# A state-space layer whose TensorE work is put in a written order, with the small products gathered in clusters and the decay differences made by broadcast loads

## The chip, the cores and the metric

The kernel runs on one core of one Trainium2 chip. The metric is the device time of one launch in microseconds (us). PE is TensorE, DVE VectorE, ACT ScalarE, POOL GpSimd, SP the engine that issues most loads.

## The reference

A network of two layers serves two requests with the same weights: a prompt of 256 tokens without history, and eight sequences of 16 tokens with caches, 384 tokens of width 1024 in all. The first layer (a short convolution beside attention) and both feed-forward parts are untouched here. The second layer is a Mamba-2 mixer: 32 heads of 64 in four groups, a state of 128, a convolution of width 4. It computes, cut to what matters:

```python
def odd_mixer(h, ...):
    z, xbc, dt_raw = split(h @ w_in)
    xbc = silu(causal_dwconv(xbc, conv_state, conv_w, conv_b))
    xs, bm, cm = split(xbc)
    dt = softplus(dt_raw + dt_bias)
    y, h_last = ssd_scan(xs, dt, -exp(a_log), bm, cm, ssm_state, chunk)
    y = (y + d_skip * xs) * silu(z)
    y = rms_norm(y per group) * norm_w
    return y @ w_out, ...

def ssd_scan(x, dt, a, bmat, cmat, h0, chunk):       # per chunk of 64, or a whole sequence of 16
    cum = cumsum(dt * a)
    decay = exp(where(tri, cum[q] - cum[s], -inf))   # per head, q and s in the chunk
    mix = (c[q] . b[s]) * decay * dt[s]
    y_intra = mix @ x
    states = sum over s of b[s] * exp(cum[last] - cum[s]) * dt[s] * x[s]
    h = exp(cum[last]) * h + states                  # from chunk to chunk
    y_inter = exp(cum[q]) * (c[q] . h_in)
```

## The kernel before

Features or tokens lie on the 128 partitions. Each dense product is made of three TensorE products (`three`): the weight and the activation are split into a rounded high part and a low rest (`wh` and `wl`, `Hh` and `Hl`), and high by high, low by high and high by low are added up in PSUM. Lines 413 to 415 of the profile are these three. Weights arrive in blocks of 128 x 1024 (512 KB) in one fixed sequence on SP's queue into three buffers (`raw`). ScalarE copies a block to `wh` (line 294), DVE subtracts to get `wl` (line 288); a block feeds 24 dense products of 384 columns. `W.take` hands out the pieces in the order of the packed file, so that order and the order of the dense products in the program have to agree.

PSUM has eight banks. In the SSM layer three of them (`pmm`) take dense products and five (`paux`) the small ones.

The layer goes through its four groups g of eight heads. For each group there are:

- *conv*: six tiles of 128 channels (`conv4`): 24 dense products named xbc each, then `pad` (DVE takes them out of PSUM), a first step of the convolution `c` on ScalarE, three on DVE, and the silu on ScalarE. Two tiles give B and C, four give x.
- *turns*: `cb` (C by B) and `bT` (B transposed) for three blocks of 128 tokens; twelve transposes xT turn x to `xt`, tokens on partitions.
- *decays*: the differences cum[q] - cum[s] of a group, four tiles of 128x512 (`td`, two blocks of 128 prompt tokens by two halves of four heads). Here they are TensorE products sg of `tdr` (made by DVE) and `ck`; ScalarE then takes relu and exp.
- *scan*: for each of three blocks of tokens `mix` (DVE: decay by cb), `xdt` (DVE) and `xw` (GpSimd), sixteen small products y of 64 columns, S (states of a prompt block) and yi (the part from the earlier state). The third block holds the eight sequences: their states `h0` (256 KB each) are loaded, give eight products yi, and new states hn, four of which fill four small banks at a time.
- *gate*: z, 72 dense products of 512 columns; `y` times silu(z), a mean square over the group, the scaling `rg`, then twelve transposes yT, split to `yh` and `yl`.
- *out*: op, 96 dense products of 384 columns, added to the residual X.

Ahead of the first group stand the step sizes: six transposes `dtt`, a softplus of some twenty small DVE instructions to `dt` and `dA`, and the products E, cT and sgS, which sum dA over the chunk.

The order in which each engine runs its instructions is made by a scheduler at build time: it places an instruction when its inputs are ready by its own costs, in program order as a tie-break. A `Fill` feeds dense products of the next group's conv, of z and of the last group's out between the scan's small ones: `fill(n)` behind a small step lets n x `FILL_O[g]` steps of three dense products go.

```python
FILL_O = (1.4, 1.5, 1.5, 0.6)
def __call__(self, n=1):
    self.due += n * self.ratio
    while self.due >= 1:
        self.due -= 1
        next(self.gen, None)
```

In the profile a name with a number, such as `y__5073`, is one buffer's use; `h__` are the loaded states, and after the group's first products S1 too.

Of the kernel before, what the change touches and what calls it, by code (L numbers as in the profile page):

```python
# [18 lines left out]
P = 128  # L19
# [8 lines left out]
FILL_O = (1.4, 1.5, 1.5, 0.6)  # L28
# [55 lines left out]
def _pack(x):  # L84
# [150 lines left out]
def build(nc, tc, d, stop=None):  # L235
    ctx = ExitStack()
    V, S, G, T = nc.vector, nc.scalar, nc.gpsimd, nc.tensor
# [101 lines left out]
    class Weights:  # L339
        def __init__(self):  # L340
            self.tiles, self.made, self.raw, self.pos = {}, 0, None, 0

            self.gain, t = {}, 32 + 3 * NF + 6
            for g in range(5):
                t += (6 if g < 3 else 0) + (4 if g < 4 else 0)
# [566 lines left out]
    o1 = od.enter_context(tc.tile_pool(name="o1", bufs=2))  # L912
    sts = o0.tile([P, 24, NB, 3], F32, name="sts")
# [79 lines left out]
    def channels(g):  # L993

        Bg, Cg = t512("B", 1, (P, NT)), t512("C", 2, (P, NT))
        yield from conv4(16 + g, Bg)
        yield from conv4(20 + g, Cg)
# [21 lines left out]
        xt = t512("xt", 2, (P, 3, 512))  # L1019
        for i in range(4):  # L1020
            xf = t512("sq", 2, (P, NT))
            yield from conv4(4 * g + i, xf)
            ps = paux("xT")
            for b in range(3):
                T.transpose(ps[:, b * P:(b + 1) * P], xf[:, b * P:(b + 1) * P], ident)
            act(xt[:, :, i * P:(i + 1) * P], ps[:, :NT].rearrange("p (b n) -> p b n", n=P), AF.Copy)
        return Cg, Cm, CB, Bt, Bm, xt
# [116 lines left out]
    class Gate:  # L1144
# [26 lines left out]
        def part(self, b):  # L1171
            y = self.ys[b]
            tt(y, y, self.got["z"][:, b, :], ALU.mult)
            if self.late:
                with tc.high_priority():
                    self.turn(b)
# [87 lines left out]
```

## Time and profile before

| | before |
|---|---|
| median of 3 runs | 1079.92 us (1077.25 to 1080.81) |
| profiled execution | 1079.71 us |
| its span in the trace | 1077.9 us |
| mean granted TensorE clock | 0.989 |
| SSM layer, first xbc to first product of the last feed-forward part | 459.16 to 795.70 us |

The span runs from the first to the last instruction of the trace; the execution's own time has the launch around it. A row of the timeline gives the start, the duration, engine, line and operation, output and inputs, partitions and elements, and in brackets how long the engine had idled and which engine's instruction let it go. In a row of grouped instructions the count, the busy sum in us and the mean of one in ns stand behind the shapes. A PE row's duration reaches past the start of the next one, since products overlap in the array; what one costs in a row of them is the distance of the starts.

### The profile page before, as it was taken

What the parts mean: (1) busy time and instruction counts of PE and PEld (TensorE: products, weight loads), DVE (VectorE), ACT (ScalarE), POOL (GpSimd) and SP (SyncE); (2) the same over time, 40 slices, a digit from 0 to 9 for tenths busy, and PEclk for the clock granted to TensorE, in tenths of its full rate; (3) what the DMA queues carried; (4) which work ended last, traced back from release to release, by engine and by line L of the source; (5) the groups of instructions that cost most, each with busy time, mean ns of one, the idle gap of its engine ahead of it and who ended that gap; (6) DMA issues with size and microseconds to landing.
All of it is one profiled execution on the core that took longest, in us unless ns stands there. A gap on an engine that the chain in (4) does not pass through costs nothing.

```text
span 1077.9 us, 16678 instructions
## 1 busy us (share of the span) xinstructions
PE 1054.0 (98%) x6332; PEld 972.6 (90%) x6332; DVE 739.3 (69%) x1321; ACT 476.5 (44%) x741; POOL 158.2 (15%) x377
## 2 busy tenths in 40 slices
PE   9999999999999999999899999999899999999998
PEld 6788899999999999988768689785899999999998
DVE  7968557777677644478889769677787677765332
ACT  6344334544444433357445545552454444444221
POOL 0030000100000000023454432324001000010000
PEclk9999999999999999999899899999899999999999
DMA  8542543344444444432444435436334344344441
GB/s 280 153 151 76 158 131 126 125 129 126 125 130 124 138 122 133 121 108 97 147 160 163 137 117 187 149 125 218 101 123 137 125 130 125 130 121 149 137 147 42
DMA packets 47944, 146.07 MB, mean 136 GB/s; under 512 B 5720, under 2 KB 7976, under 8 KB 47864
## 3 DMA queue, kind: packets, MB, share of 16 engines
q1 hardware_dynamic: 41976, 132.55, 38.9%
q10 hardware_dynamic: 4608, 8.39, 2.0%
q0 software_dynamic: 1280, 4.06, 1.0%
q8 instruction: 50, 0.82, 0.3%
q14 instruction: 30, 0.25, 0.1%
HBM read 131.61 MB, written 13.37 MB: 135 GB/s over the span
## 4 chain that ended last, share of the span: by engine, by line
PE 45%; DVE 8%; ACT 2%; issue 1%; DMA 1%; ACTq 0%; DVEq 0%; POOL 0%
PE fg L413 3%; PE fg L414 3%; PE fd L414 3%; PE fd L415 3%; PE fd L413 3%; PE fg L415 3%; PE fa L415 3%; PE fa L414 3%; PE fa L413 3%; DVE c L291 2%; PE z L413 2%; PE xbc L414 2%; PE z L414 2%; PE xbc L415 2%; PE xbc L413 2%; PE z L415 2%
## 5 line engine op out<-in xcount | busy, mean ns | idle before, releaser
L288 DVE TENSOR_TENSOR wl<-raw,wh 128x1024 fp32r<-128x1024 f32 (+1 forms) x205 | 252.1, 1231 | 134.7 <-ACT wh L294 134.0
L294 ACT ACTIVATE wh<-raw 128x1024 fp32r<-128x1024 f32 (+1 forms) x205 | 216.1, 1055 | 232.7 <-PE fd L414 95.0
L413 PE MATMUL fg<-Hh,wh 128*128 128x384 f32 x352 | 118.5, 337 | 1.1 <-DVE pad L288 0.8
L414 PE MATMUL fg<-Hl,wh 128*128 128x384 f32 x352 | 118.7, 337 | 0.0
L413 PE MATMUL fa<-Hh,wh 128*128 128x384 f32 x352 | 118.6, 337 | 0.0
L414 PE MATMUL fa<-Hl,wh 128*128 128x384 f32 x352 | 118.4, 336 | 0.1
L415 PE MATMUL fa<-Hh,wl 128*128 128x384 f32 x352 | 118.4, 336 | 0.0
L415 PE MATMUL fg<-Hh,wl 128*128 128x384 f32 x352 | 118.3, 336 | 0.0
L413 PE MATMUL fd<-hh,wh 128*128 128x384 f32 x352 | 118.3, 336 | 0.0
L415 PE MATMUL fd<-hh,wl 128*128 128x384 f32 x352 | 118.3, 336 | 0.0
L414 PE MATMUL fd<-hl,wh 128*128 128x384 f32 x352 | 118.3, 336 | 0.0
L291 DVE SCALAR_TENSOR_TENSOR c<-pad,prm,c 128x400 f32<-128x400 f32 (+1 forms) x160 | 103.5, 654 | 6.9 <-ACT c L294 5.1
L413 PEld LDWEIGHTS fg<-Hh,wh 128*128 128x128 f32 x352 | 66.2, 188 | 1.7 <-ACT R L294 1.1
L413 PE MATMUL xbc<-Hh,wh 128*128 128x384 f32 x192 | 66.4, 346 | 0.7 <-DVE X L288 0.7
L414 PE MATMUL xbc<-Hl,wh 128*128 128x384 f32 x192 | 66.7, 347 | 0.0
L414 PEld LDWEIGHTS fa<-Hl,wh 128*128 128x128 f32 x352 | 66.2, 188 | 0.5 <-DVE Hl L291 0.4
L415 PEld LDWEIGHTS fg<-Hh,wl 128*128 128x128 f32 x352 | 66.2, 188 | 0.1
L415 PE MATMUL xbc<-Hh,wl 128*128 128x384 f32 x192 | 66.3, 345 | 0.0
L413 PEld LDWEIGHTS fa<-Hh,wh 128*128 128x128 f32 x352 | 66.2, 188 | 0.1
L414 PEld LDWEIGHTS fg<-Hl,wh 128*128 128x128 f32 x352 | 66.2, 188 | 0.1
L414 PEld LDWEIGHTS fd<-hl,wh 128*128 128x128 f32 x352 | 66.2, 188 | 0.0
L415 PEld LDWEIGHTS fa<-Hh,wl 128*128 128x128 f32 x352 | 66.2, 188 | 0.0
(808 smaller groups left out, 2141.2 us busy)
## 6 DMA issues: line engine op xcount, KB each, us to landing
raw<-w SPq DMA_DIRECT2D x219, 512.0 KB, 3.5
kc<-kc SPq DMA_DIRECT2D x8, 256.0 KB, 3.5
vc<-vc SPq DMA_DIRECT2D x8, 256.0 KB, 3.0
X<-x SPq DMA_DIRECT2D x8, 192.0 KB, 3.8
o_y<-X SPq DMA_DIRECT2D x8, 192.0 KB, 2.7
o_v<-vt POOLq DMA_DIRECT2D x3, 256.0 KB, 2.5
o_k<-kraw POOLq DMA_DIRECT2D x3, 256.0 KB, 3.3
cst<-cst SPq DMA_DIRECT2D x1, 617.0 KB, 6.0
```

Source lines behind the costliest of these rows:

```text
L288: (eng or V).tensor_tensor(out=out, in0=a, in1=b, op=op)
L291: V.scalar_tensor_tensor(out=out, in0=a, scalar=s, in1=b, op0=op0, op1=op1)
L294: S.activation(out, a, f, **kw)
L413: T.matmul(out, lhsT=ah, rhs=bh, start=start, stop=False)
L414: T.matmul(out, lhsT=ah, rhs=bl, start=False, stop=False)
L415: T.matmul(out, lhsT=al, rhs=bh, start=False, stop=stop)
```

## The change

- `FILL_O` and the filling of the SSM layer go. A wrapper around TensorE keeps products and transposes in the program's order (`keep_in_program_order`) from the first turn of x to the end of the layer, and the program is written out as that order.
- For each of the first three groups the small products stand in five clusters with dense runs between: yT of the group before, S and y of all three blocks (`within`) / 24, 48 or 72 xbc / yi, cb, bT (`before`, `turn_bc`) / 24 xbc / four hn / 24 xbc / four hn / z (behind 24 more xbc in group 2) / xT / 48 xbc or 96 op. The last group alternates with pieces of z and op.
- The weight blocks are packed in the new order: B and C of a group apart from its x.
- The decays: cum is copied from PSUM (`cumK` per token, `cumQ` per head), `cumQ` goes to a DRAM tile `rows`, and each td is loaded by a DMA on SP's queue that repeats four rows of 128 on all partitions (256 KB written); GpSimd subtracts `cumK`. `tdr`, `cq`, `ck` and the sixteen sg go.
- The mix of the two prompt blocks is made in place in td; `xt` has one buffer, and yi and S1 are kept in it. Adding yi to y and the skip product move to GpSimd for three groups (the skip product was there before). The mean square's scratch is `yi`.

```diff
-FILL_O = (1.4, 1.5, 1.5, 0.6)
...
-    def chan(g):
-        fm(wi, (4096 + P * g, 4608 + P * g))
+    def bc(which, g):
+        fm(wi, (4096 + 512 * which + P * g,))
+    def xs(g):
         fm(wi, range(2048 + 512 * g, 2560 + 512 * g, P))
...
-    chan(0)
+    bc(0, 0), bc(1, 0), xs(0), bc(0, 1), bc(1, 1)
     for g in range(4):
+        if g == 2:
+            bc(0, 3), bc(1, 3)
         if g < 3:
-            chan(g + 1)
+            xs(g + 1)
         tm(wi, 512 * g)
+        if g == 0:
+            bc(0, 2), bc(1, 2)
         if g:
             out(g - 1)
...
+    class Tensor:
+        keep = False
+        def matmul(self, *a, **kw):
+            ins = nc.tensor.matmul(*a, **kw)
+            if self.keep:
+                tc.keep_in_program_order(ins)
...
+    T = Tensor()
...
-    cq = o0.tile([P, 2, P], F32R, name="cq")
-    ck = o0.tile([P, 2, P], F32R, name="ck")
-    V.memset(f32(cq[64:128, :, :]), 1.0)
-    V.memset(f32(ck[0:64, :, :]), 1.0)
+    cumK = o0.tile([P, 64], F32, name="cumK")
+    V.tensor_copy(cumK, ps[:, 0:64])
...
-    cs = ps[0:32, 0:256].rearrange("p (b q) -> p b q", q=P)
-    act(cq[0:32, :, :], cs, AF.Copy)
-    tt(cq[32:64, :, :], cs, f32(cq[0:32, :, :]), ALU.subtract)
-    act(ck[64:96, :, :], cs, AF.Copy, scale=-1.0)
-    V.tensor_scalar_mul(ck[96:128, :, :], f32(cq[32:64, :, :]), -1.0)
+    cumQ = o1.tile([32, 256], F32, tag="pad", name="cumQ")
+    V.tensor_copy(cumQ, ps[0:32, 0:256])
+    rows = dram.tile([2, 32, P], F32, name="rows")
+    nc.sync.dma_start(out=rows.rearrange("b h q -> h b q"), in_=cumQ.rearrange("h (b q) -> h b q", q=P))
...
+        return Cg, Cm, CB, Bt, Bm
+    def turn_x(xs):
+        xt = t512("xt", 1, (P, 3, 512))
+        for b in range(3):
             ps = paux("xT")
-            for b in range(3):
-                T.transpose(ps[:, b * P:(b + 1) * P], xf[:, b * P:(b + 1) * P], ident)
-            act(xt[:, :, i * P:(i + 1) * P], ps[:, :NT].rearrange("p (b n) -> p b n", n=P), AF.Copy)
-        return Cg, Cm, CB, Bt, Bm, xt
+            for i in range(4):
+                T.transpose(ps[:, i * P:(i + 1) * P], xs[i][:, b * P:(b + 1) * P], ident)
+            act(xt[:, b, :], ps, AF.Copy)
+        return xt
...
     def decays(g):
-        sg, out = [], []
+        out = []
         for b in range(2):
             for hf in range(2):
                 c0 = 8 * g + 4 * hf
-                td = o1.tile([P, 4, P], F32R, tag="tdr", name="tdr", bufs=2)
-                tt(td, f32(cq[:, b, :]).unsqueeze(1).broadcast_to([P, 4, P]),
-                   C("hsel")[:, c0:c0 + 4].unsqueeze(2).broadcast_to([P, 4, P]), ALU.mult)
-                ps = paux("sg")
-                T.matmul(ps, lhsT=ck[:, b, :], rhs=td.rearrange("p h q -> p (h q)"), start=True, stop=True)
                 dec = t512("td", 4, (P, 4, P))
-                act(dec.rearrange("p h q -> p (h q)"), ps, AF.Relu, scale=-1.0)
+                nc.sync.dma_start(out=dec, in_=rows[b, c0:c0 + 4, :].partition_broadcast(P))
+                tt(dec, dec, cumK[:, 32 * b + c0:32 * b + c0 + 4].unsqueeze(2).broadcast_to([P, 4, P]), ALU.subtract, G)
+                act(dec, dec, AF.Relu, scale=-1.0)
                 out.append(dec)
         for dec in out:
             act(dec, dec, AF.Exp, scale=-1.0)
...
+    class Group:
...
+            self.mix, self.xdt, self.xw, self.ys = [decs[0:2], decs[2:4]], [], [], []
+            for b in range(2):
+                for half in self.mix[b]:
+                    tt(half, half, self.CB[:, b, :].unsqueeze(1).broadcast_to([P, 4, P]), ALU.mult)
...
+                xdt = t512("xdt", 3)
+                tt(heads(xdt[:, :]), x3, bc64(self.col(dt, b)), ALU.mult)
...
+                tt(heads(xw[:, :]), x3, bc64(self.col(wdt, b)), ALU.mult, G)
...
+        def skip(self):
...
+                y = t512("y", 5)
+                tt(heads(y[:, :]), heads(self.xt[:, b, :]), bc64(prr("dsk", 32)[:, self.h8]), ALU.mult, G)
+                self.ys.append(y)
...
+        def within(self):
...
+            for b in range(3):
+                if b < 2:
+                    ph = paux("S")
+                    T.matmul(ph, lhsT=self.Bt[:, b, :], rhs=self.xw[b], start=True, stop=True)
+                    if b == 0:
...
+                py = paux("y")
...
+                        T.matmul(py[q, 64 * h:64 * h + 64], lhsT=self.mix[b][h // 4][:, h % 4, q],
+                                 rhs=self.xdt[b][:, 64 * h:64 * h + 64], start=True, stop=True)
+                tt(self.ys[b], self.ys[b], py, ALU.add)
+            self.h0 = []
+            for bb in range(NB):
+                h0 = t512("h0", 8)
+                nc.sync.dma_start(out=h0, in_=d["h0"][bb, g])
+                self.h0.append(h0)
...
+        def before(self, late):
...
+                yi = self.xt[:, b, :]
+                tt(heads(yi), heads(pi[:, :]), bc64(self.col(E, b)), ALU.mult)
+                tt(self.ys[b], self.ys[b], yi, ALU.add, None if late else G)
...
+        def states(self, par):
...
+            ph = [paux("hn") for _ in range(4)]
...
+                T.matmul(ph[i], lhsT=self.Bm[rows, par, :], rhs=self.xw[2][rows, :], start=True, stop=True)
...
+                tt(heads(h0[:, :]), heads(h0[:, :]), bc64(E[:, o:o + 8]), ALU.mult, G)
+                tt(h0, h0, ph[i], ALU.add)
+                nc.scalar.dma_start(out=d["o_hs"][bb, self.g], in_=h0)
...
+        def part(self, b, zs):
...
+            tt(y, y, zs[:, b, :], ALU.mult)
+            act(t512("yi", 1), y, AF.Square, accum_out=self.ssq[:, b:b + 1])
...
     decs = decays(0)
-    cur, out = run(channels(0)), None
-    for g in range(4):
-        got = {}
-        def beside_scan():
-            if g < 3:
-                got["next"] = yield from channels(g + 1)
-            got["z"] = yield from project_z()
-            if g:
-                yield from add_out(*out)
-        fill = Fill(beside_scan(), FILL_O[g])
-        gate = Gate(fill, got, g == 3)
-        decs = scan(fill, gate, g, decs, *cur)
-        if "z" not in got:
-            fill.rest()
-        gate(None, None)
-        now = gate.end()
-        fill.rest()
-        out, cur = now, got.get("next")
...
+    T.keep = True
+    xt = turn_x(xs)
+    grp = Group(0, decs, bc_, xt)
+    grp.skip()
+    Cn = conv_bc(1, 1)
+    xs = [conv_x(1, 0)]
+    out = None
+    for g in range(3):
+        grp.within()
+        decs = decays(g + 1)
+        if g == 2:
+            Bn, Cn = conv_bc(0, 3), conv_bc(1, 3)
+        if g:
+            xs = [conv_x(g + 1, 0)]
+        if g < 2:
+            xs.append(conv_x(g + 1, 1))
+        grp.before(False)
+        bc_ = turn_bc(g + 1, Bn, Cn)
+        if g == 2:
+            xs.append(conv_x(g + 1, 1))
+        else:
+            xs.append(conv_x(g + 1, 2))
+        grp.states(0)
+        xs.append(conv_x(g + 1, len(xs)))
+        grp.states(1)
+        if len(xs) < 4:
+            xs.append(conv_x(g + 1, 3))
+        zs = run(project_z())
+        gate = Gate(grp.ys, False)
+        for b in range(3):
+            gate.part(b, zs)
+        xt = turn_x(xs)
+        gate.factor()
+        nxt = Group(g + 1, decs, bc_, xt)
+        if g == 0:
+            Bn, Cn = conv_bc(0, 2), conv_bc(1, 2)
+        else:
+            run(add_out(*out, None))
+        for b in range(3):
+            gate.turn(b)
+        out, grp = gate.y2, nxt
+        grp.skip()
+    grp.within()
+    z = project_z()
+    steps(z, 12)
+    grp.before(True)
+    zs = steps(z)
+    gate = Gate(grp.ys, True)
+    for b in range(3):
+        gate.part(b, zs)
+    grp.states(0)
+    op = add_out(*out, None)
+    steps(op, 12)
+    grp.states(1)
+    gate.turn(0)
+    steps(op, 12)
+    for b in (1, 2):
+        gate.turn(b)
+    steps(op)
     nc.gpsimd.dma_start(out=d["o_sm"], in_=osm)
-    run(add_out(*out))
+    run(add_out(*gate.y2, gate.factor()))
+    T.keep = False
```

TensorE at the end of group 0 and the start of group 1 (yT turns the gated y of group 0, S and y belong to group 1, xbc to a later conv) has this order before the change:

```order
L415 MATMUL xbc<-Hh,wl 128x384
L596 MATMUL yT<-cst,y__4976 128x128 x4
L413 MATMUL xbc<-Hh,wh 128x384
L596 MATMUL yT<-cst,y__5073 128x128 x4
L414 MATMUL xbc<-Hl,wh 128x384
L596 MATMUL yT<-cst,y__5267 128x128 x4
L1084 MATMUL y<-xdt__5641,mix__5647 64x64 x16
L1123 MATMUL S<-xw__5643,Bt__5132 128x512
L415 MATMUL xbc<-Hh,wl 128x384
```

Each turn is followed by a dense product, and S and y are spread between dense ones. After the change TensorE has at that place:

```order
L249 MATMUL xbc<-Hh,wl 128x384
L254 MATMUL yT<-cst,y__5023 128x128 x4
L254 MATMUL yT<-cst,y__5025 128x128 x4
L254 MATMUL yT<-cst,y__5027 128x128 x4
L249 MATMUL S<-xw__5598,Bt__5292 128x512
L249 MATMUL y<-xdt__5596,td__5200 64x64 x8
L249 MATMUL y<-xdt__5596,td__5204 64x64 x8
L249 MATMUL S<-xw__5602,Bt__5292 128x512
L249 MATMUL y<-xdt__5600,td__5208 64x64 x8
L249 MATMUL y<-xdt__5600,td__5212 64x64 x8
L249 MATMUL y<-xdt__5604,mix__5608 64x64 x16
L249 MATMUL xbc<-Hh,wh 128x384
```

Dense products no longer stand between the transposes, and the y products of blocks 0 and 1 read td itself; the yT rows follow a run of dense ones in which no other small product stands.

ScalarE around the decays of the next group (td: relu and exp; wh: weight copies; c4: first step of a conv; sq and xf: its silu) has this order before the change, in group 0, for group 1:

```order
L294 ACTIVATE td__5221<-sg_5219 128x512
L294 ACTIVATE td__5227<-sg_5225 128x512
L294 ACT_TABLE_LOAD
L294 ACTIVATE td__5221<-td__5221 128x512
L294 ACTIVATE wh_5436<-raw_5434 128x1024
L294 ACTIVATE td__5233<-sg_5231 128x512
L294 ACTIVATE td__5239<-sg_5237 128x512
L294 ACTIVATE td__5227<-td__5227 128x512
L294 ACTIVATE td__5233<-td__5233 128x512
L294 ACTIVATE td__5239<-td__5239 128x512
L294 ACTIVATE c4_5295<-pad4_5288,prm_74 128x408
L294 ACTIVATE c4_5346<-pad4_5339,prm_74 128x408
```

Relu reads the PSUM bank of sg there. After the change ScalarE has, in group 1, for group 2:

```order
L315 ACTIVATE td__5808<-td__5808 128x512
L315 ACT_TABLE_LOAD
L315 ACTIVATE td__5808<-td__5808 128x512
L315 ACTIVATE td__5812<-td__5812 128x512
L315 ACTIVATE td__5816<-td__5816 128x512
L315 ACTIVATE td__5820<-td__5820 128x512
L315 ACTIVATE td__5812<-td__5812 128x512
L315 ACTIVATE wh_5957<-raw_5955 128x1024
L315 ACTIVATE td__5816<-td__5816 128x512
L315 ACTIVATE td__5820<-td__5820 128x512
L315 ACTIVATE c4_5867<-pad4_5860,prm_74 128x408
L315 ACTIVATE wh_6023<-raw_6021 128x1024
```

Relu now reads td itself instead of PSUM, and the first conv step c4 stands behind all eight steps of the decays.

DVE at the end of the step-size chain (lp to dA; c4 and pad4 are conv work) has this order before the change:

```order
L291 SCALAR_TENSOR_TENSOR c4_4739<-pad4_4732,prm_74,c4_4739 128x408
L291 SCALAR_TENSOR_TENSOR lp_4583<-lp_4581,lr_4571 128x96
L291 SCALAR_TENSOR_TENSOR c4_4739<-pad4_4732,prm_74,c4_4739 128x408
L291 SCALAR_TENSOR_TENSOR lp_4585<-lp_4583,lr_4571 128x96
L291 SCALAR_TENSOR_TENSOR c4_4739<-pad4_4732,prm_74,c4_4739 128x408
L291 SCALAR_TENSOR_TENSOR lp_4587<-lp_4585,lr_4571 128x96
L291 SCALAR_TENSOR_TENSOR c4_4804<-pad4_4797,prm_74,c4_4804 128x408
L288 TENSOR_TENSOR wl_4923<-raw_4920,wh_4922 128x1024
L291 SCALAR_TENSOR_TENSOR lu_4589<-lp_4587,lz_4569 128x96
L291 SCALAR_TENSOR_TENSOR c4_4804<-pad4_4797,prm_74,c4_4804 128x408
L291 SCALAR_TENSOR_TENSOR dt_4533<-lu_4589,mxx_4591 128x96
L291 SCALAR_TENSOR_TENSOR c4_4804<-pad4_4797,prm_74,c4_4804 128x408
```

Conv steps and a wl alternate with the chain. After the change DVE has there:

```order
L312 SCALAR_TENSOR_TENSOR lp_4587<-lp_4585,lr_4573 128x96
L312 SCALAR_TENSOR_TENSOR lp_4589<-lp_4587,lr_4573 128x96
L312 SCALAR_TENSOR_TENSOR lu_4591<-lp_4589,lz_4571 128x96
L312 SCALAR_TENSOR_TENSOR dt_4535<-lu_4591,mxx_4593 128x96
L312 SCALAR_TENSOR_TENSOR dA_4536<-dt_4535,ea_4596 128x96
L309 TENSOR_TENSOR h0__4599<-dA_4536,cst_75 128x256
L309 TENSOR_TENSOR h0__4621<-dA_4536,cst_75 128x512
L995 COPY cumK_4611<-E_4601 128x64
L309 TENSOR_TENSOR wdt_4538<-E_4537,dt_4535 128x96
L1000 COPY cumQ_4616<-cT_4613 32x256
L309 TENSOR_TENSOR pad4_4678<-xbc_4647,R_79 128x256
L309 TENSOR_TENSOR pad4_4678<-xbc_4647,R_79 128x8x16
```

The conv steps that stood between the chain's instructions now stand behind it, cumK, wdt and cumQ.

More of the change, by code (lines that the diff above doesn't have):

```diff
@@ L341, in __init__ @@
             self.tiles, self.made, self.raw, self.pos = {}, 0, None, 0
[L343 removed]
+            self.gain, t = {}, 32 + 3 * NF + 8
             for g in range(5):
[L345 removed]
+                t += (4 + 4 + 2, 4 + 4, 2 + 4 + 4, 4, 0)[g]
                 if g:
@@ L991, in build, with conv_x, conv_bc, turn_bc @@
     act(decS, ps, AF.Exp)
[L993 to L997, printed above, removed]
+    def conv_x(g, i):
+        out = t512("xf", 4, (P, NT))
+        run(conv4(4 * g + i, out))
+        return out
+    def conv_bc(which, g):
+        out = t512("BC"[which], 1 + which, (P, NT))
+        run(conv4(16 + 4 * which + g, out))
+        return out
+    def turn_bc(g, Bg, Cg):
         ps = paux("cb")
@@ new lines, in build @@
+    decs = decays(0)
+    bc_ = [conv_bc(0, 0), conv_bc(1, 0)]
+    xs = [conv_x(0, 0)]
+    bc_ = turn_bc(0, *bc_)
+    xs += [conv_x(0, i) for i in (1, 2, 3)]
+    Bn = conv_bc(0, 1)
+    T.keep = True
[18 more added lines that the diff above has]
+            xs.append(conv_x(g + 1, 1))
+        else:
+            xs.append(conv_x(g + 1, 2))
[6 more added lines that the diff above has]
+        gate = Gate(grp.ys, False)
+        for b in range(3):
+            gate.part(b, zs)
[4 more added lines that the diff above has]
+            Bn, Cn = conv_bc(0, 2), conv_bc(1, 2)
+        else:
+            run(add_out(*out, None))
+        for b in range(3):
+            gate.turn(b)
+        out, grp = gate.y2, nxt
+        grp.skip()
```

190 lines of the change are left out of this document (71 added, 119 removed).

## The prediction

> **What bounds the kernel now.** I read the page first, then the chain of waits of TensorE, the windows of the SSM stage and its timeline.
>
> ```profile
> span 1077.9 us, 16678 instructions
> PE 1054.0 (98%) x6332; PEld 972.6 (90%) x6332; DVE 739.3 (69%) x1321; ACT 476.5 (44%) x741; POOL 158.2 (15%) x377
> ```
>
> TensorE is busy for 98% of the span, so only its idle time, its slow time and its order can be won. The change touches the stage between these two rows:
>
> ```profile
> 459.16 0.41 PE L413 MATMUL xbc<-Hh,wh 128*128 128x384 f32 x1 [0.74 <-DVE X L288]
> ...
> 795.70 0.34 PE L413 MATMUL fa<-Hh,wh 128*128 128x384 f32 x1
> ```
>
> 795.70 − 459.16 = 336.5 us. The next view gives busy us and count of PE, PEld, DVE, ACT, POOL, then TensorE's granted clock; the three lines behind it show TensorE alone in stretches at half clock.
>
> ```profile
> 459.00:796.00 337.00, 323.11 (x1988) 269.62 (x1989) 270.64 (x492) 171.42 (x305) 111.55 (x166) 0.97 0.42 142
> 517.40:524.20 6.80, 6.18 (x40) 0.50 0.86 308
> 613.00:619.80 6.80, 6.78 (x13) 0.50 0.73 231
> 756.30:763.10 6.80, 5.00 (x20) 0.50 0.64 208
> ```
>
> DVE works 271 of 337 us, 80%: whatever TensorE waits for is mostly queued there. At half clock the busy 6.18 + 6.78 + 5.00 = 18.0 us hold 9.0 us of full-speed work, so 9.0 us are lost. What TensorE waits for:
>
> ```profile
> PE y L1084 <- DVE mix__5075 L288: 3.2, 2, 2.5
> PE yT L596 <- DVE h__7491 L288: 2.5, 1, 2.5
> PE yT L596 <- DVE yi__7567 L288: 1.4, 1, 1.4
> PE sg L1042 <- DVE tdr L288: 1.3, 2, 0.7
> PE xT L1025 <- ACT sq__5358 L294: 1.2, 1, 1.2
> ...
> PE cb L1001 <- ACT C__6481 L294: 0.2, 1, 0.2
> ```
>
> The twelve rows of that answer, less X's 0.7 that lies ahead of the stage, come to 13.3 us.
>
> **What the change takes away.** Stepping between kinds of work and the products that go:
>
> ```profile
> L1042 PE MATMUL sg<-tdr,ck 128*128 128x512 f32 x16 | 7.0, 466 | 1.3 <-DVE tdr L288 1.3
> 561.58 0.39 PE L415 MATMUL z<-wh,Hl 128*128 128x512 f32 x1
> 561.81 0.34 PE L413 MATMUL xbc<-Hh,wh 128*128 128x384 f32 x1
> 561.98 0.34 PE L414 MATMUL xbc<-Hl,wh 128*128 128x384 f32 x1
> ...
> 574.14 0.66 PE L596 MATMUL yT<-cst,y__4976 128*128 128x128 f32 x4
> 574.55 0.42 PE L413 MATMUL xbc<-Hh,wh 128*128 128x384 f32 x1
> 574.81 0.60 PE L596 MATMUL yT<-cst,y__5073 128*128 128x128 f32 x4
> 577.60 0.74 PE L415 MATMUL xbc<-Hh,wl 128*128 128x384 f32 x1
> 578.18 0.34 PE L413 MATMUL xbc<-Hh,wh 128*128 128x384 f32 x1
> ```
>
> - Starts of dense products lie 0.17 us apart at 384 columns, 0.23 at 512. The sixteen sg (512 columns, overlapped in the pipe) are worth 16 × 0.23 = 3.7 us; their summed busy time, 7.0, is the upper end.
> - A dense step beside small products costs more: 574.55 to 574.81 is 0.26 (0.09 over), 577.60 to 578.18 is 0.58 (0.41 over). My mean over the stage is 0.19 a run of small products. There are 64 such runs between dense ones; the new order has 28. 36 × 0.19 = 7.0 us; ends 36 × 0.09 = 3.2 and 36 × 0.41 = 14.8.
> - The new-state products hn wait for free PSUM banks inside a run, which the waits do not list:
>
> ```profile
> 744.70 1.14 PE L1108 MATMUL hn<-xw__7384,Bm__6616 32*128 32x512 f32 x8
> 612.40 2.79 PE L1108 MATMUL hn<-xw__5967,Bm__5134 32*128 32x512 f32 x3
> ```
>
> A clean set of four (eight passes) takes 1.14; the second row shows three passes taking 2.79. The eight sets take 15.5 us start to start against 8 × 1.07, so 7.0 us of waiting.
>
> With all waits gone the stage would be 336.5 − 3.7 − 7.0 − 13.3 − 7.0 − 9.0 = 296.5 us. DVE also loses sixteen tdr products; the small products themselves are not fewer or shorter. The moved weight blocks are the same bytes on the same queue: nothing.
>
> **What it puts back.** With a fixed order TensorE cannot pass a late small product, so every lateness behind the cover is a wait.
>
> *Startup.* The dt chain on DVE runs from the transposes to dA:
>
> ```profile
> 469.75 0.86 PE L473 MATMUL dtt<-cst,dts 128*128 128x32 f32 x6
> 470.65 0.57 DVE L291 SCALAR_TENSOR_TENSOR dx<-dtt,r,prm 128x32 f32<-128x32 f32 x3 [2.11 <-PE dtt L473]
> 474.03 1.22 DVE L288 TENSOR_TENSOR wl<-raw,wh 128x1024 fp32r<-128x1024 f32 x1
> 476.04 0.74 DVE L323 RECIPROCAL lr<-la 128x96 f32<-128x96 f32 x1
> 485.30 0.29 DVE L291 SCALAR_TENSOR_TENSOR dA<-dt,ea 128x96 f32<-128x96 f32 x1
> 485.64 0.41 PE L966 MATMUL E<-dA,cst 128*128 128x32 f32 x2 [0.91 <-DVE dA L291]
> ```
>
> Now 81 xbc (14.1 us) cover the 15 us; then 72 xbc stand ahead of E in all, 32 of them behind dtt, so TensorE is dry at 470.4 + 32 × 0.174 = 476.0. On DVE only three wl (3 × 1.2) and no conv work stand among the chain's own 5 us of small instructions; with ScalarE's steps it ends near 479.8. Wait 3.8, and 1.2 more until pad4_4678, now behind cumK, wdt and cumQ on DVE, frees a bank: 5.0. Ends: 0, if DVE were ready, and 9.3, if the chain kept its 15 us. The half clock followed idles of 2.5 us in the stretches above, so I add 2.5.
>
> *Decays, three groups.* The broadcast into td (256 KB) can start only when the y products have read the old td; then four GpSimd subtractions in a row, and ScalarE's relu and exp stand ahead of wh and of the next conv's first step, so conv and evacuation on DVE come late, hn's banks and the next cb with them.
>
> ```profile
> 514.17 2.02 POOL L288 TENSOR_TENSOR y__5267<-xt__4764,prm 128x512 f32<-128x512 f32 x1
> 621.12 1.04 POOL L288 TENSOR_TENSOR h__6181<-h__6181,E 128x512 f32<-128x512 f32 x1 [6.89 <-PE yi L1101]
> 530.97 1.28 ACT L294 ACT_TABLE_LOAD   x1
> 532.26 0.64 ACT L294 ACTIVATE td__5221<-td__5221 128x512 f32<-128x512 f32 x1
> 536.14 0.68 DVE L288 TENSOR_TENSOR mix__5647<-td__5221,CB__5125 128x512 f32<-128x512 f32 x1
> 554.92 1.53 DVE L288 TENSOR_TENSOR y__5267<-y__5267,yi__5578 128x512 f32<-128x512 f32 x1
> h__5377<-h SPq DMA_DIRECT2D x1, 256.0 KB, 3.8
> ```
>
> Chain: 3.8 (a 256 KB load) + 4 × 1.04 + relu 0.64 + table 1.28 + 4 × 0.64 = 12.4 us behind the last y. Cover in dense work: 24 xbc (4.2 us) ahead of the second cluster in group 0, 48 and 72 in the next two, and 24 xbc between each of the following clusters. The lower end is that none of it shows (0), the upper that the 12.4 us less 4.2 show in every group (24.6). On SP's queue td's loads stand ahead of raw and h0 loads and hold them while they wait for y; three raw buffers of 24 dense products each cover 3 × 4.2 = 12.5 us, so I count nothing for it, and nothing for their 4 MB beside the stage's 337 us × 142 GB/s = 48 MB. I take 7.0 over the three, what hn waits for banks now, and 3.5 for the second cluster of group 2, whose cb needs a C convolved just then.
>
> *From group 0 to group 1.* z ends at 561.81 and its yT starts at 574.14: 12.3 us of gate, mean square and scale, covered by 69 xbc. Afterwards xT (1.1) and 48 xbc (8.3) cover 9.4, while DVE has the mix and xdt products of the next group and the same wl as well: I put yT 1.7 later than now (a wl of 1.2 and a small step), at 14.0, so 4.6 late, and a half-clock stretch (6.8 × 0.5 = 3.4) behind it: 8.0. Ends: 2.9, if yT keeps its 12.3 and the clock holds, and 12, if two more products of 1.53 stand ahead of it and the clock falls. Groups 1 and 2 have 96 op (16.7 us): nothing.
>
> *Smaller.* xT of group 0 waits for ScalarE's last silu, 1.0 (as sq__5358 above, 1.2); op's wh behind the scaling of y on ScalarE, 2 × 0.9; cluster 1 wants five aux banks in a row, 3 × 0.5; the last gate 1.0, in place of the 2.5 and 1.4 above. Together 5.3. GpSimd's added sums hide under 48 or more dense products.
>
> Sum: 7.5 + 7.0 + 3.5 + 8.0 + 5.3 = 31.3. Stage 296.5 + 31.3 = 327.8, gain 8.7. The profiled execution took 1079.71 (median 1079.92, 0.02% off): 1079.7 − 8.7 = **1071 us**.
>
> The Trainium skill, "SBUF — State Buffer" (section on SBUF's two separate sides), says that VectorE with two SBUF inputs and a GpSimd operation that reads SBUF take a shared port in turn, as a lock for the whole instruction. The trace agrees in size: the same 128x512 product takes 0.68 or 1.53 on DVE, 1.04 or 2.02 on GpSimd. By that rule the new GpSimd work is a loss for DVE too; the third rival prices it from the rows.
>
> **Rivals.**
> - *Cushion.* Three mm banks and three weight buffers absorb all but the startup and the turn to group 1: 296.5 + 7.5 + 8.0 = 312.0, gain 24.5, 1055 us. For it: ScalarE is only half busy (171 of 337). Against: DVE at 80%.
> - *Half clock in each group.* The clusters are long runs of short products and each ends in a wait; if each of three groups drops the clock once, 3 × 3.4 = 10.2: 1081 us, no change. For it: all three stretches above began at such places. The Trainium skill, "TensorE: Matmul & The Clock Gate" (Why this matters), puts the drop at idle gaps over some 3 us; this trace shows it dropped after 2.5, and the measurement decides; by that rule this rival would be dearer to reach and the charge of 2.5 at the startup would stay.
> - *GpSimd late* (slower). Each subtraction takes 2.02, not 1.04, since DVE works beside it: the chain is 4 × 0.98 = 3.9 later in three groups, 11.8, and with the clock falling in each, 10.2, it is 1071 + 22 = 1093 us. It decides from 8.7 / 3 = 2.9 a group without the clock, a subtraction of 1.77. For it: 271 us of DVE work; against: sixteen tdr leave DVE.
>
> **How the numbers follow.** Forecast 0.42 (1061 to 1077), cushion 0.18, half clock 0.16, GpSimd late 0.24. Below 1052 I leave 0.08, above 1089 0.12, so the range is 1052 to 1089: its ends lie near the cushion and between the two slow cases. A change under 0.3% (3.2 us) can hardly be told from none here. Faster 0.60, same 0.16, slower 0.24.
>
> **What the profile after would show.** No sg and fewer than 30 small runs between dense ones; an idle of 3 to 5 us ahead of E, released by dA; yT of group 0 late by 4 to 5 us behind rg; hn sets longer than 1.14 or a cb that waits for C; and the clock at 0.50 behind the longest of these. I am wrong if td's broadcasts land much later than 3.8 us (they share SP's queue with the weights), if GpSimd's subtractions are near 2 us, or if the idle sum stays under 15 us.

## The result, and the profile after

The changed kernel takes 1117.07 us (median; 1114.3 to 1119.4) against 1080.11 in the runs beside it: ratio 1.0346, 95% interval 1.0316 to 1.0377. It is 37 us slower, where 8.7 us less were forecast (1071). The page of the changed kernel:

```profile
span 1117.5 us, 16676 instructions
PE 1059.1 (95%) x6316; PEld 979.4 (88%) x6316; DVE 750.8 (67%) x1297; ACT 478.3 (43%) x737; POOL 183.0 (16%) x399
PEclk9999999999999999988988899899999999999999
```

TensorE has 16 products fewer, the sg, and yet idles 5% instead of 2% of a longer span. The SSM stage runs from 461.20 to 835.44 us, 374.2 us against 336.5 (the remaining 2 us lie ahead of it, where runs of the unchanged part differ by as much). The first line is its window (start and end, length, busy us and count of PE, PEld, DVE, ACT and POOL, TensorE's clock, share and GB/s of the DMA engines); then TensorE alone in the seven stretches at half clock:

```profile
459.00:836.00 377.00, 329.95 (x1983) 277.58 (x1982) 282.50 (x468) 174.20 (x301) 137.24 (x188) 0.92 0.43 139
480.40:490.60 10.20, 8.45 (x27) 0.51 0.55 189
508.10:514.90 6.80, 5.37 (x20) 0.52 0.25 78
521.50:524.90 3.40, 3.40 (x13) 0.50 0.29 114
558.90:569.10 10.20, 7.56 (x16) 0.51 0.80 246
596.50:603.30 6.80, 5.54 (x34) 0.51 0.29 117
633.90:644.10 10.20, 7.15 (x13) 0.51 0.65 215
705.10:715.30 10.20, 4.19 (x16) 0.54 0.12 46
```

41.7 us of busy time at half clock cost 20.8 us; before it was 9.0. What TensorE waits for in the stage (total, times, longest):

```profile
PE cb L249 <- ACT C__6580 L315: 8.6, 1, 8.6
PE xbc L249 <- DVE pad L309: 7.0, 1, 7.0
PE hn L249 <- DVE h__5792 L309: 6.8, 1, 6.8
PE hn L249 <- DVE h__5184 L309: 5.8, 1, 5.8
PE op L249 <- ACT wh L315: 5.3, 3, 2.0
PE yT L254 <- ACT y__5023 L315: 4.3, 1, 4.3
PE E L249 <- DVE dA L312: 3.9, 1, 3.9
PE xT L254 <- ACT xf__4894 L315: 2.9, 1, 2.9
PE z L249 <- DVE pad L309: 1.1, 1, 1.1
```

With op's 0.5 for wl these are 46.2 us, against 13.3. So the balance of the stage is: waits +32.9, half clock +11.8, hn's waits inside its runs 7.6 against 7.0, and the forecast gains (sg 3.7, fewer switches 7.0) taken off: +34.6 of the measured +37.7. The rest is not assigned.

Two places show how the waits come about. The first is behind the second cluster of group 0: DVE, GpSimd, then TensorE's wait. The timeline gives start, duration, instruction; rows are left out between those shown.

```profile
549.49 1.52 DVE L309 TENSOR_TENSOR td__5208<-td__5208,CB__5285 128x512 f32<-128x512 f32 x1
552.39 1.42 DVE L312 SCALAR_TENSOR_TENSOR c<-pad,prm,c 128x408 f32<-128x408 f32 x1
553.73 2.30 DVE L309 TENSOR_TENSOR mix__5608<-CB__5285,decS 128x1024 f32<-128x1024 f32 x1
557.63 1.72 DVE L309 TENSOR_TENSOR wl<-raw,wh 128x1024 fp32r<-128x1024 f32 x1
560.82 0.67 DVE L309 TENSOR_TENSOR h__5184<-h__5184,hn 128x512 f32<-128x512 f32 x1
...
547.53 1.49 POOL L309 TENSOR_TENSOR h__5184<-h__5184,E 128x512 f32<-128x512 f32 x1
550.43 1.49 POOL L309 TENSOR_TENSOR h__5192<-h__5192,E 128x512 f32<-128x512 f32 x1
553.33 1.62 POOL L309 TENSOR_TENSOR y__5027<-y__5027,xt__4986 128x512 f32<-128x512 f32 x1
554.91 2.02 POOL L309 TENSOR_TENSOR h__5186<-h__5186,E 128x512 f32<-128x512 f32 x1
560.22 1.38 POOL L309 TENSOR_TENSOR h__5198<-h__5198,E 128x512 f32<-128x512 f32 x1
561.54 3.27 PE L249 MATMUL hn<-xw__5019,Bm__4797 32*128 32x512 f32 x6 [5.85 <-DVE h__5184 L309]
```

While GpSimd works through its products, the DVE instructions with two SBUF inputs shown here take 1.4 to 2.3 times their time (a conv step 0.63 alone, 1.42 here; wl 1.21 and 1.72; td × CB 0.68 and 1.52), and GpSimd's products 1.38 to 2.02 instead of 1.04. The add to h__5184, which has one input in PSUM, keeps its 0.67 beside GpSimd. This add, which frees a bank for hn, stands behind all of these on DVE, at 560.82, though its GpSimd product had ended at 549.02, and TensorE has stood for 5.85 us.

The second place is group 2's second cluster: SP, GpSimd, ScalarE, DVE, TensorE.

```profile
684.25 0.42 SPq L1066 DMA_DIRECT2D td__6514<-rows  x1
689.44 1.04 POOL L309 TENSOR_TENSOR td__6514<-td__6514,cumK 128x512 f32<-128x512 f32 x1 [4.69 <-DMA td__6514<-rows]
690.51 0.63 ACT L315 ACTIVATE td__6514<-td__6514 128x512 f32<-128x512 f32 x1 [6.91 <-POOL td__6514 L309]
696.54 0.61 ACT L315 ACTIVATE td__6526<-td__6526 128x512 f32<-128x512 f32 x1
697.06 0.71 ACT L315 ACTIVATE c<-pad,prm 128x408 f32<-128x408 f32 x1
703.61 8.34 DVE L312 SCALAR_TENSOR_TENSOR c<-pad,prm,c 128x408 f32<-128x408 f32 x6
710.64 0.62 ACT L315 ACTIVATE C__6580<-c 128x256 f32<-128x256 f32 x2 [6.78 <-DVE c L312]
711.11 1.65 PE L249 MATMUL cb<-C__6580,B__6534 128*128 128x128 f32 x6 [8.64 <-ACT C__6580 L315]
```

ScalarE stands 6.91 us in front of relu, since the broadcast has not landed; the first conv step is behind the eight steps of the decays, at 697.06, though DVE had written its pad by 692.09. DVE's conv and C follow, and cb is 8.64 us late. A part of this is the first cause again: the six conv steps at 703.61 take 8.34 us beside GpSimd's y sum and h0 × E, where six in a row take 3.48 in the run cumq_own below. ScalarE's queue does the same in the startup: E waits 3.9 as forecast, and then the banks wait for a pad copy that stands on DVE behind a conv step, which stands on ScalarE behind the first decays (7.0). The startup lies ahead of the point from which TensorE's order is kept, so the written order is not the cause there.

### The profile page after: what moved, and what is told of

Same layout as the page of the kernel before. It is cut to its first block, busy times and chain, and to the rows that moved or that the text cites. A ratio compares the mean times of both kernels' runs of the same rounds, so it can differ in the third digit from the quotient of the medians.

```text
span 1117.5 us, 16676 instructions
## 1 busy us (share of the span) xinstructions
PE 1059.1 (95%) x6316; PEld 979.4 (88%) x6316; DVE 750.8 (67%) x1297; ACT 478.3 (43%) x737; POOL 183.0 (16%) x399
## 4 chain that ended last, share of the span: by engine, by line
PE 67%; DVE 10%; issue 2%; ACT 2%; DMA 0%; POOL 0%; ACTq 0%; DVEq 0%; SPq 0%
PE fd L249 16%; PE fg L249 16%; PE fa L249 15%; PE z L249 6%; PE op L249 4%; PE xbc L249 4%; DVE c L312 3%; DVE wl L309 1%; PE hn L249 1%; PE y L249 1%; ACT wh L315 1%; PE yi L249 1%; PE S L249 1%; PE yT L254 1%; DVE pad L309 0%
## 5 line engine op out<-in xcount | busy, mean ns | idle before, releaser
L312 DVE SCALAR_TENSOR_TENSOR c<-pad,prm,c 128x400 f32<-128x400 f32 (+1 forms) x160 | 113.6, 714 | 11.8 <-ACT c L315 9.9
L249 PE MATMUL xbc<-Hh,wh 128*128 128x384 f32 x192 | 69.4, 361 | 7.7 <-DVE pad L309 7.0
L249 PEld LDWEIGHTS fd<-hh,wh 128*128 128x128 f32 x352 | 66.2, 188 | 0.0
```

The lines of the kernel that those rows point to most:

```text
L249: ins = nc.tensor.matmul(*a, **kw)
L312: V.scalar_tensor_tensor(out=out, in0=a, scalar=s, in1=b, op0=op0, op1=op1)
```

## The experiments

Ratios are to the kernel before, with 95% intervals; "less" and "more" without a second name are against the changed kernel's 1117.1.

**Theories.** A, shared port: GpSimd's products (h0 × E, y's sum) and DVE slow each other. B, ScalarE's queue: DMA-fed decays stand ahead of conv work. C, the written order itself, with too little cover for what is late. D, the cumQ buffer: it is a "pad", one of the two through which all conv work goes, so the dt chain stands ahead of the convs.

**order_only** and **decay_only** split the change. The first is the new order with the sg products and tdr kept (for room, tdr and the gate's square lie in xdt's three buffers; in the kernel before tdr has two of its own), the second the kernel before with cumK, cumQ and the new `decays()` (one piece of y2 moves from tdr's buffers to those of `sq`).

> The new order with the decays made as before (tdr on DVE, sg on TensorE; the gate's square uses an xdt buffer, for room). Decay queue (relu and exp of late broadcasts stand at the head of ScalarE's queue and hold the next conv's first step): the 7.0 us wait of xbc for pad in the startup and the 8.6 of cb for C in group 2 go with the half clock behind them, sixteen sg cost 3.7, so about 1117 - 20 + 4 = 1100 us. Shared port (DVE and GpSimd take turns at 128x512 products): the hn waits of 6.8 and 5.8 stay, since the states' products are still GpSimd's, so not under 1095. Written order itself: nothing much changes, 1112 to 1117.

> The kernel before with the new decays alone (broadcast loads, GpSimd subtraction). Decay queue: ScalarE waits here too, 1085 to 1095 us against 1080. Shared port: four more GpSimd products a group, 1080 to 1086. Written order itself: 1076 to 1081, because the sg products and tdr go and the scheduler can move around a late decay.

order_only: 1124.2, 1.0415 [1.0389, 1.0440]. decay_only: 1100.0, 1.0204 [1.0179, 1.0230]. decay_only lies above every range expected, order_only above all but the port's, which was open upwards. Each half loses by itself, +45 and +21 us; together they lose 37, less than their sum. In the new order the new decays are worth some 7 us against order_only: TensorE no longer waits for tdr. How much of that wait comes from the buffers that tdr shares with xdt there was not tried, so the 45 us are not the written order's alone. The largest waits of order_only, then of decay_only:

```profile
PE sg L249 <- DVE tdr L309: 8.1, 3, 3.5
PE yT L254 <- ACT y__5033 L315: 4.9, 1, 4.9
```

```profile
PE cb L999 <- ACT C__4647 L294: 8.6, 1, 8.6
PE E L967 <- DVE dA L291: 3.9, 1, 3.9
```

decay_only shows E's wait and the late C of the startup where TensorE keeps the scheduler's order: they belong to the decays and cumQ's buffer, not to the order of TensorE.

**no_h0mul** leaves GpSimd's 32 products h0 × E out (the old state is added undecayed); **h0_on_dve** does them on DVE.

```diff
-tt(heads(h0[:, :]), heads(h0[:, :]), bc64(E[:, o:o + 8]), ALU.mult, G)
+tt(heads(h0[:, :]), heads(h0[:, :]), bc64(E[:, o:o + 8]), ALU.mult)   # h0_on_dve
```

> The changed kernel without the 32 GpSimd products of the loaded states by their decay (the old state goes into the new one undecayed). Shared port: DVE's steps behind the second cluster fall from 1.4-1.5 to 0.65, the hn waits of 6.8 and 5.8 go with the half clock behind them, 1117 - 16 = 1101 us. Decay queue: DVE is late because conv is late, the waits shrink by 2 or 3 us, 1112 to 1116. Written order: 1117.

> The changed kernel with the 32 products of the loaded states by their decay on DVE in place of GpSimd. Shared port: DVE gets 32 x 0.68 = 22 us more work, but its other steps fall from 1.4-1.5 back to 0.65 where GpSimd ran beside them; the hn waits shrink to a few us: 1101 to 1106 us against 1117. Decay queue alone: DVE is only later, 1118 to 1124.

no_h0mul: 1098.3, 1.0177 [1.0151, 1.0203]: 18.8 less; hn's wait for h__5184 is 0.4, that for h__5792 is gone, and cb's 8.6 is 5.1. h0_on_dve: 1103.6, 1.0229 [1.0212, 1.0246]: 13.5 less, with the same arithmetic. The place of the first wait in h0_on_dve:

```profile
551.16 1.21 DVE L309 TENSOR_TENSOR wl<-raw,wh 128x1024 fp32r<-128x1024 f32 x1
554.29 0.63 DVE L312 SCALAR_TENSOR_TENSOR c<-pad,prm,c 128x408 f32<-128x408 f32 x1
555.99 0.68 DVE L309 TENSOR_TENSOR h__5190<-h__5190,E 128x512 f32<-128x512 f32 x1
...
552.33 3.21 PE L249 MATMUL hn<-xw__5019,Bm__4797 32*128 32x512 f32 x8
```

No wait ahead of hn (the set still takes 3.21 instead of 1.14, since it waits for banks inside), conv steps at 0.63, wl at 1.21 instead of 1.72. The window of the stage (DVE is the third busy time, GpSimd the fifth):

```profile
459.00:820.00 361.00, 327.38 (x1974) 276.99 (x1975) 281.51 (x499) 173.86 (x301) 99.06 (x156) 0.94 0.44 144
```

DVE took over 32 products of 0.68 us, 22 us, and its busy time is 281.5 against 282.5 (750.3 and 750.8 over the whole span): what it does more, it saves in the time of its other instructions. That shows A.

**sub_on_act** takes the subtractions from GpSimd (relu with cumK as its bias); **late_exp** leaves them and emits relu and exp later, those of group 0 at the end of the startup and those of groups 1 to 3 ahead of the z of the group before.

```diff
+for i in range(4): act(dec[:, i, :], dec[:, i, :], AF.Relu, scale=-1.0, bias=cumK[:, n:n + 1])   # sub_on_act, n = 32*b + c0 + i
...
 decays(g)                     # late_exp: loads and subtractions only
+decay_acts(out)               # relu and exp, ahead of T.keep = True and of zs = run(project_z())
```

> The changed kernel with the subtraction made by ScalarE: relu(cumK - cumQ) per head of 128 with cumK as the bias, so four short relu in place of one, and no GpSimd step. Decay queue: the chain is shorter by four GpSimd steps (4 to 5 us) and longer by some 4 x 0.6, so the pad and C waits fall by 2 to 3 us each, 1110 to 1114. Shared port: the hn waits stay, no more than 2 us from less GpSimd work: 1115. Written order: 1117.

> The changed kernel with relu and exp of the decays written behind the conv work (ahead of xT in group 0, ahead of z in the others), so that the scheduler prefers a conv's first step; the broadcasts and subtractions stay where they are. Decay queue: the 7.0 wait for pad goes, and of the 8.6 for C where the scheduler lets c4 pass, with the half clock behind: 1100 to 1106 us. Shared port: the pad wait goes, hn waits stay, 1107 to 1111. No part of ScalarE's queue: 1115 to 1119.

sub_on_act: 1116.9, 1.0362 [1.0337, 1.0388], the same. GpSimd's subtraction is not the cost; the chain is shorter, but ScalarE still stands in front of it, and the wait turns up elsewhere (cb for C 8.8 in the startup). late_exp: 1108.7, 1.0279 [1.0260, 1.0298], 8.4 less: the startup's pad wait of 7.0 is gone from the list, and cb's 8.6 is 1.3. That shows B, though not at the 11 to 17 us expected of it: waits of 2.8 (cb for C) and 2.6 (xT) appear in the startup instead.

**late_exp_h0_y_dve** is late_exp with h0 × E and y's sums on DVE, to see whether A and B add.

```diff
+tt(self.ys[b], self.ys[b], yi, ALU.add)   # always on DVE
```

> Late relu and exp, and on DVE the states' products and the added yi. Both causes together: what the two single runs gain, 25 to 30 us in all: 1087 to 1092 us. Where one cause hides behind the other the sum is less than the parts: 1096 to 1102. DVE as the new bound (20 us more of its own work): above 1105.

1092.5, 1.0125 [1.0090, 1.0161]: 24.6 less, more than 8.4 + 13.5 = 21.9 (y's sums are in it too, and the interval is some 4 us to either side). They add.

**cumq_own** and **decay_only_cumq** give cumQ another buffer, in the changed kernel and in decay_only.

```diff
-cumQ = o1.tile([32, 256], F32, tag="pad", name="cumQ")
+cumQ = t512("S0", 1)[0:32, 0:256]
```

> The changed kernel with cumQ in a buffer of its own (S0, unused until group 0's scan) in place of one of the two pad buffers of the conv. In the built order the conv's steps then stand between the instructions of the step-size chain again and E behind 81 xbc instead of 32. If the shared buffer is the startup's cause: the E wait of 3.9, the pad wait of 7.0 and their half clock go, 15 to 18 us: 1099 to 1103. If the decays themselves are (late broadcasts ahead of the conv on ScalarE): cb waits for C in the startup in place of pad, 8 us stay: 1107 to 1111.

> The kernel before with the new decays, and cumQ in its own buffer. If the shared buffer made decay_only slow (1100 against 1079): 1077 to 1083. If the late decays on ScalarE did: 1092 to 1100.

cumq_own: 1111.3, 1.0303 [1.0287, 1.0319], 5.8 less. decay_only_cumq: 1090.6, 1.0103 [1.0088, 1.0119], 9.4 less than decay_only and between the two ranges expected. E's wait is 0.8 in cumq_own, and the pad wait is gone; but most of it comes back in one piece:

```profile
PE xT L254 <- ACT xf__4894 L315: 12.6, 1, 12.6
```

The conv of this tile starts behind the first decays on ScalarE (its pad is written by 500.46, its first step runs at 508.41), so B takes what D frees. D is shown, in the startup alone.

**z_earlier** puts z of group 0 a cluster earlier, as cover for its gate; **all_mended** has late_exp, h0 and y on DVE, cumQ's buffer and this together; **x_turn_later** is all_mended with more dense work ahead of the turn of X.

```diff
+grp.states(0); zs = run(project_z())              # z_earlier, group 0; B(0,2), C(1,2) later
...
+Cn = conv_bc(1, 1); grp.turn_x()                  # x_turn_later; z split by steps(z, 12)
```

> The changed kernel with group 0's z (and its weight blocks) ahead of the last 24 xbc and the second hn, and the first 24 xbc of the following conv ahead of xT, so that 72 xbc, hn and xT stand between z and yT instead of 48 xbc and xT. If cover alone is missing there: the yT wait of 4.3 and the half clock behind it (in all 7 to 8 us) go, 1109 to 1111. If DVE's backlog at that place sets it: the wait moves to hn or z, 1113 to 1118.

> All of it: late relu and exp, the states' products and the added yi on DVE, cumQ in its own buffer, z of group 0 earlier. From late_exp_h0_y_dve (1092) less 15 to 18 for the startup and 7 for yT: 1068 to 1071, faster than before (1079) by 0.8 to 1%. If the waits only move, 1075 to 1082.

> all_mended with 24 more xbc (C of group 1) ahead of group 0's xT, one more conv tile ahead of the first S and y, and z of group 0 split around its first hn. If the xT wait of 9.5 is a lack of cover: 4.2 us less, about 1080 to 1081, level with before. If DVE's backlog sets the pace there (the added xbc bring their own conv work to DVE): the wait moves to xT, S or hn again and the time stays at 1084 to 1087.

z_earlier: 1114.9, 1.0324 [1.0308, 1.0340], 2.1 less. The cover is there, but TensorE now waits at z for a pad (10.2) and at S for yl (4.7), both from DVE. all_mended: 1085.1, 1.0052 [1.0039, 1.0066], above both ranges expected. x_turn_later: 1086.7, 1.0068 [1.0053, 1.0083], no better. What all_mended still waits for:

```profile
PE xT L255 <- ACT xf__4886 L316: 9.5, 1, 9.5
PE S L250 <- DVE yl L310: 4.7, 1, 4.7
PE op L250 <- ACT wh L316: 4.6, 3, 2.0
PE z L250 <- DVE pad L310: 3.6, 1, 3.6
```

With the edits for A, B and D 32 of the 37 us are back, and the forecast gain is still not there: waits remain wherever dense work is moved to. A and B are not wholly gone either. GpSimd still makes the subtractions, xw and skip products. And the silu of the xT wait, xf__4886, runs at 509.91 on ScalarE, behind a relu that stood 1.74 us for GpSimd, an exp, and two loads of a function table (ACT_TABLE_LOAD) at 1.28 each, though DVE had ended its conv at 507.67. Such loads come with each change between exp and silu in the rows here: 18 in this stage, 12 in the changed kernel's, 10 before.

**mended_less_dve**, **before_less_dve**, **after_less_dve** leave two of three conv steps on DVE out, in all_mended, before and after: is it DVE's load that the order cannot cover?

```diff
-for t in (1, 2, 3):
+for t in (3,):
```

> all_mended without two of the three DVE steps of each of the 24 conv tiles (48 x 0.64 = 31 us of DVE work left out, the conv is not the reference's). If DVE is the bound behind its waits: the waits of 9.5 (xT), 4.7 (S) and 3.6 (z) go, 1066 to 1070. If ScalarE or the loads are: 1080 to 1085.

> The kernel before with the same two conv steps left out. If its greedy order already hides DVE: 1075 to 1080. If its 13 us of waits come from DVE's load as well: 1066 to 1072, and the written order is no better than this with DVE relieved.

> The changed kernel with the same two conv steps left out. DVE's load as the cause of the hn waits and of what lies behind: 1117 - 20 = 1097 or lower. ScalarE's queue alone: 1110 to 1115.

1075.8, 0.9973 [0.9957, 0.9989]; 1067.5, 0.9891 [0.9878, 0.9904]; 1101.1, 1.0211 [1.0196, 1.0226]. The first and the last lie between their ranges. The same relief is worth 9.3, 11.4 and 16.0 us. The changed kernel has the most to gain, but even so the written order stays behind the scheduler's (1075.8 against 1067.5). DVE's load is a part of C, not the whole of it.

**before_h0_dve**, **before_h0_xw_dve**, **before_no_gpsimd_512** take A to the kernel before: h0 × E on DVE, then xw too, then the skip product too.

```diff
-tt(heads(h0[:, :]), heads(h0[:, :]), bc64(E[:, o:o + 8]), ALU.mult, G)
+tt(heads(h0[:, :]), heads(h0[:, :]), bc64(E[:, o:o + 8]), ALU.mult)
+tt(heads(xw...), x3, bc64(col(wdt, b)), ALU.mult)       # xw, without G
+... bc64(prr("dsk", 32)[:, h8]), ALU.mult)              # skip, without G
```

> The kernel before with the 32 products of the loaded states by their decay on DVE in place of GpSimd. Shared port, as h0_on_dve showed it for the changed kernel: DVE's own busy time stays where it is, hn's bank waits (7 us over 8 x 1.07) shrink, 1072 to 1077. If the greedy order already runs other work in these gaps: 1077 to 1081. DVE as the bound with 22 us more work: 1084 to 1090.

> As before_h0_dve, with the twelve xw products on DVE too (12 x 0.69 = 8 us more). If taking GpSimd off the port is free for DVE: another 0 to 3 us less. If not: 2 to 5 more, since xw is on the way to S and hn.

> As before_h0_xw_dve, with the twelve skip products (x by D) on DVE as well, so that GpSimd has no 128x512 product left in the layer; 8 us more of DVE's own work. If the port stays the larger cost: 1064 to 1068. If DVE's own load now counts, since the skip products were early and off the path on GpSimd: 1068 to 1073.

1073.7, 0.9943 [0.9927, 0.9959]; 1068.2, 0.9887 [0.9871, 0.9903]; 1067.2, 0.9889 [0.9867, 0.9911]. The second beats both kernels, by 1.1% and by 4.4%, and gains 5.5 us on the first, where 0 to 3 were expected; the skip product adds nothing that can be measured. The stage of the kernel before, then that of before_h0_xw_dve in the same window, and its longest wait:

```profile
459.00:785.00 326.00, 312.11 (x1926) 258.66 (x1927) 260.13 (x472) 164.06 (x293) 111.55 (x166) 0.97 0.43 143
```

```profile
459.00:785.00 326.00, 317.07 (x1986) 265.07 (x1987) 281.57 (x535) 170.71 (x304) 54.27 (x122) 0.99 0.45 147
```

```profile
PE yT L596 <- DVE h__7491 L288: 2.7, 1, 2.7
```

In before_h0_xw_dve DVE does 63 instructions more in the same time and is busy 21 us more, and GpSimd is busy 57 us less; more work is done (TensorE 60 products more) and the clock is 0.99. The longest wait of its TensorE, in the row above, is 2.7.

## Why the prediction was wrong, point by point

The step that failed is the term for the decays, 7.0 over three groups and 3.5 for group 2's second cluster. It was sized by hn's waits of today, near its lower end. Measured, start to start, are two sets of hn that take 10.2 and 12.2 us instead of 1.07 each, together 20.3 us more, and 8.6 at the second cluster: 28.9 instead of 10.5, above the upper end of 24.6 that had been given. The half clock behind these waits, 9.5 us, was not in the term at all.

Its mechanism was half right. The conv did stand behind the decays on ScalarE, as the term says (late_exp). But it took hn's lateness for the decays' and put GpSimd's products at h0 and y at nothing: hn's waits of 5.8 and 6.8 fall to 0.4 and nothing when h0 × E is left out and the decays stay as they are (no_h0mul), and cb's shrinks from 8.6 to 5.1.

With each wait's half clock counted to it, the sum of 31.3 reads about 75 in the trace: the startup 17.8 instead of 7.5, the decays' term about 38 instead of 10.5, the turn to group 1 7.1 instead of 8.0, the smaller ones 11.5 instead of 5.3. So the decays' term is 28 of the 46 us by which the stage (374.2) is over the forecast (327.8).

- *Taken away.* sg is gone and small runs are fewer, as forecast. The 3.7 and 7.0 us were not measured by themselves; the balance above closes to 3 us with them, which bears them out no more closely than that.
- *Startup, E.* 3.8 forecast, 3.9 measured, by the cover as worked out; on DVE the chain has two wl and a wait of 1.06 for ScalarE in place of the three wl, so a part of the match is luck. What stands behind it was wrong: 7.0 us for a pad instead of 1.2. The price looked at cumK, wdt and cumQ on DVE and not at ScalarE, whose queue holds relu and exp ahead of the conv.
- *Turn to group 1.* 4.6 and 3.4 forecast, 4.3 and about 2.8 measured (a stretch of 6.8 with 5.5 us of work at half clock).
- *Smaller.* xT 2.9 instead of 1.0; op's wh 5.3 instead of 1.8; cluster 1's banks 0 instead of 1.5. "GpSimd's added sums hide" does not hold: they run beside DVE's late work (1.62 instead of 1.04 in the rows above) while hn's adds wait there, but no run moves them alone.
- *Half clock.* 20.8 us against 5.9 put back. The second rival had one drop a group and 10.2 us; there are seven stretches, two of them in the startup.
- *Third rival.* It had the side and the mechanism (port shared by DVE and GpSimd, 1093) but not the place. The subtractions take 1.03 to 1.49, but for one of 2.02 in the startup, and moving them changed nothing (sub_on_act); the cost is in the eight products h0 × E and the sums of a cluster (1.29 to 2.02 in group 0), which the written order puts at one spot together with DVE's td × CB, mix and conv steps. The Trainium skill, "SBUF — State Buffer" (SBUF: two separate sides), says that the operation which starts first keeps the shared port and the other blocks wholly. The rows agree: 0.63 becomes 1.42, and h0_on_dve's DVE time is no longer.
- *Cushion.* Three banks and three weight buffers did not absorb it: 46.2 us of waits.

Open: with the edits for the three mechanisms the written order is still 5.5 us behind the kernel before, 11 us behind the kernel before with h0 × E on DVE as well (1073.7), and 8 us behind it with DVE relieved. The remaining waits (xT 9.5, S 4.7, op 4.6, z 3.6) would account for it, since a fixed order cannot pass a late product, but it is not shown that the order is their cause. No run put the scheduler's order and the written one side by side with nothing else changed: order_only also has the written clusters on the other engines and tdr in xdt's buffers. And in every run the scheduler places the other engines' instructions anew, so a few us of each difference can be its doing.

## What to carry to other kernels

Here, with TensorE 98% busy, a written order had little to gain, and each product that was late by 2.9 us or more became a wait with a half-clock stretch behind it; before clustering, list for each cluster the last producer on every in-order queue, and what that queue holds ahead of it. Try work fed by a DMA behind what is ready already on its queue (8.4 us here), and count the table loads that it brings on ScalarE. And a product of two SBUF inputs given to GpSimd to spare DVE did not spare it: the 32 here cost DVE nearly what it needs to make them itself in the changed kernel, half of that in the kernel before. Try it on DVE first.

## What the runs showed of the hardware

- Taking 32 products of 128x512 from GpSimd to DVE left DVE's busy time as it was in the changed kernel (282.5 and 281.5 us in the stage; without the products it is 731.5 instead of 750.8 over the span). In the kernel before the same move made DVE 11.1 us busier (739.3 to 750.4) for 22 us of work, so about half was spared there by GpSimd. The mean of a conv step shows the same (count, busy us, mean ns), in the kernel after, before, and before_h0_xw_dve:

```profile
L312 DVE SCALAR_TENSOR_TENSOR c<-pad,prm,c 128x408 f32<-128x408 f32 x72 | 58.0, 814 | 7.9 <-ACT c L315 7.5
```

```profile
L291 DVE SCALAR_TENSOR_TENSOR c<-pad,prm,c 128x408 f32<-128x408 f32 x72 | 48.0, 680 | 3.2 <-ACT c L294 2.9
```

```profile
L291 DVE SCALAR_TENSOR_TENSOR c<-pad,prm,c 128x408 f32<-128x408 f32 x72 | 45.2, 639 | 6.4 <-ACT c L294 6.3
```

- The half-clock stretches are 3.4, 6.8 or 10.2 us long. They lie behind waits of 2.9 (the xT wait, stretch from 521.5) to 8.6 us; op's waits of up to 2.0 had none behind them. The clock cost a third as much as the waits it came from (11.8 and 32.9 us more than before).
- A broadcast of four rows to 256 KB took 3.1 to 5.8 us from issue to landing in the changed kernel (median 4.8); its plain loads of that size for h0 took 2.6 to 6.6 (median 3.7).
